# An encoder layer on one core: feed-forward in two phases with its inner activations in DRAM, down projection summed whole in PSUM

## The chip, the cores and the metric

The kernel runs on one core of one Trainium2 chip. The metric is device time in microseconds (us) of one execution. Engines: TensorE (PE, with its weight loads as PEld), VectorE (DVE), ScalarE (ACT), GpSimd (POOL) and SyncE (SP), which issues every DMA of this kernel.

## What is computed

One encoder layer on two inputs with shared weights: a sample of 512 tokens (S) and a prompt of 1,024 tokens (P), width 1,024, all float32.

```
mod = silu(c) @ w_mod + b_mod                       # sh1, sc1, gt1, sh2, sc2, gt2, one vector per input
h = rmsnorm(x, g_norm1) * (1 + sc1) + sh1
q, k, v, xr, gate = split(h @ w_in)                 # 512, 128, 128, 512, 512
attn = banded_attention(q, k, v, sink)              # 8 heads, blocks of 128, window 128
lru = rglru_bidir(xr, ...) * gelu(gate)             # convolution, gates, forward and backward scan
x = x + gt1 * (concat(rmsnorm(attn), rmsnorm(lru)) @ w_out)
h = rmsnorm(x, g_norm2) * (1 + sc2) + sh2
g_, u_ = split(h @ w_ffn_in)                        # 2 x 2816 columns
x = x + gt2 * ((silu(g_) * u_) @ w_ffn_out)
y = rmsnorm(x, g_final)
```

## The kernel before

**Layout and arithmetic.** Activations are held transposed, 128 channels by 512 tokens in a tile; 512 tokens are a chunk, so S has one and P two. To keep float32 accuracy each operand of a large product is split into a high part (float32r) and a low part, `lo = x - hi`, and a product is three matmuls of 128x512: high by high, high by low, low by high (`mm3`). ACT (or DVE, as `Either` picks) makes the high part, DVE the low part. A weight tile is 128x1024 (512 KB): it is loaded into one of 3 stages (`wst`), split into `whi` and `wlo` (10 buffers) and used by 24 matmuls for each chunk. 8 k-blocks of 128 make up the width; the feed-forward has 22 blocks of 128 inner channels (NFF = 22).

**Order of work.** The program is written out at build time. A main generator issues the matmuls of the large products; after each few matmuls `Side.weave` lets other work in: the drains of finished PSUM tiles (`side.soon`, kept in a fast list), one step each of weight load, high and low split (`Weights.pump`), then steps of side generators (norms, modulation chunks `mod_chunk`, attention, `lru`). A step is issued when a cost model (`Plan`) says that its inputs are there at the time that PE has reached, and none while the model has ACT, DVE or POOL far behind PE (`behind`). `Side.finish` issues all that is left of a side generator before the main one goes on; nothing of the main work is issued in that time. Each engine then runs its instructions in that order.

**The stages.** `start` (modulation chunks 0 to 3, S's first norm), `z_main(0)` (h @ w_in of S, 14 weight tiles) beside P's first norm and the modulation chunks 4 to 9, `z_main(1)` (the same for P, both chunks for each weight tile) beside S's recurrence and attention, which are two side generators; after 11 of its tiles both are finished, S's `mixnorm` runs beside two more, then `out_main(0)` (S's product with w_out), the last z tile beside S's `norm2`, and the feed-forward of S. Beside that run P's attention, then P's `lru`, then `mixnorm` of P's first chunk, one after the other in one side generator. They are finished, and `out_main` of P's chunks, `norm2` and the feed-forward of P follow, with the final norm (`final`) at the end of each chunk.

**The feed-forward before** (`ffn`, `ffn_steps`) goes through the inner blocks once. A step "in" makes gate and up of one block (48 matmuls for each chunk), and `gate` and `up` drain them, the product `sg` is split into `ach` and `acl`, in SBUF. After every two blocks a step "out" multiplies them with their two tiles of w_ffn_out, for each of the 8 output blocks m into a fresh PSUM bank, and `drain` adds the part to x, which stays in SBUF:

```
self.dve.scalar_tensor_tensor(out=x, in0=ps, scalar=self.modT[:, seq, 40 + m:41 + m], in1=x,
                              op0=ALU.mult, op1=ALU.add)
```

That is 11 x 8 drains for a chunk. The last step of P's second chunk is done in two halves of 256 tokens, so that the final norm of the first half runs beside the matmuls of the second. PSUM has 8 banks: 4 for the main work (`pm`), 4 for the side work (`ps`).

## Time and profile before

| | |
|---|---|
| median of 3 runs | 1746.13 us (1744.09 to 1746.81) |
| the profiled execution | 1742.62 us, of which the span from first to last instruction is 1740.8 us |
| mean granted clock of TensorE | 0.978 |
| busy share of the span | PE 95%, PEld 76%, DVE 61%, ACT 40%, POOL 5% |
| moved by DMA | 166.84 MB, mean 96 GB/s |

The busy time of PE is that of pipelined matmuls: one of 128x512 takes 0.39 us from start to end, and starts 0.23 us after the one before. How fast PE works is therefore read from how many matmuls a stretch holds, not from its busy share alone. All lines of code carry the number of one helper, so groups are told apart by the names of their tiles: `pm` is a PSUM tile of the main work, `ps` one of the side work.

### The profile page before, as it was taken

The numbers are of one execution on the slowest core, as the hardware profiler recorded it, in microseconds if no ns is written. First come the engines' busy times: TensorE is split into PE (matmuls) and PEld (weight loads), VectorE is DVE, ScalarE is ACT, GpSimd is POOL, SyncE is SP. The second block draws the span as 40 slices with busy tenths as digits, with TensorE's granted clock in tenths as the row PEclk, the third lists the DMA queues.
The fourth block names the chain that finished last, engine by engine and source line by source line (L and its number), as shares of the span: only waits on it lengthen the run. The fifth ranks groups of instructions, "written<-read, shape, count | busy, mean of one in ns | idle before, by whom it ended". The sixth has DMA issues, their size and how long they took to land.

```text
span 1740.8 us, 19699 instructions
## 1 busy us (share of the span) xinstructions
PE 1651.2 (95%) x7428; PEld 1329.8 (76%) x7428; DVE 1058.5 (61%) x1733; ACT 694.9 (40%) x1135; POOL 95.7 (5%) x164
## 2 busy tenths in 40 slices
PE   7979999998999999999929999999999999999996
PEld 2656888786888887777717888888888888888885
DVE  5764876747887878787899754244244244244257
ACT  3343787525665555745735341111111111111114
POOL 0000111001222100000000000000000000000004
PEclk9988999999999999999959999999999999999999
DMA  8766322244222223233315311111111111111102
GB/s 304 266 249 212 109 91 97 86 144 158 96 63 84 73 91 127 85 115 108 104 37 188 118 46 49 49 49 49 49 49 49 49 49 49 49 49 49 49 0 97
DMA packets 70302, 166.84 MB, mean 96 GB/s; under 512 B 7360, under 2 KB 15808, under 8 KB 70208
## 3 DMA queue, kind: packets, MB, share of 16 engines
q1 hardware_dynamic: 70208, 165.59, 28.3%
q8 instruction: 58, 0.95, 0.2%
q14 instruction: 36, 0.29, 0.1%
HBM read 148.26 MB, written 17.30 MB: 95 GB/s over the span
## 4 chain that ended last, share of the span: by engine, by line
PE 82%; DVE 8%; ACT 4%; DMA 4%; issue 1%; SPq 0%; POOL 0%; POOLq 0%; DVEq 0%; ACTq 0%
PE pm L85 74%; PE ps L85 8%; DVE x L85 1%; DMA mst<-w_mod 1%; ACT ga L85 1%; DVE wlo L85 1%; DVE bc L85 1%; DVE lh L85 1%; DMA wst<-w_in 1%; ACT gs L85 1%; ACT gi L85 1%; DVE hl L85 1%; SPq L85 0%; DVE yo L85 0%; ACT whi L85 0%
## 5 line engine op out<-in xcount | busy, mean ns | idle before, releaser
L85 PE MATMUL pm<-hh,whi 128*128 128x512 f32 x1392 | 551.3, 396 | 1.6 <-ACT hh L85 1.3
L85 PE MATMUL pm<-hl,whi 128*128 128x512 f32 x1392 | 545.0, 391 | 3.5 <-DVE hl L85 3.5
L85 PE MATMUL pm<-hh,wlo 128*128 128x512 f32 x1392 | 544.9, 391 | 2.1 <-DVE wlo L85 2.1
L85 PEld LDWEIGHTS pm<-hh,whi 128*128 128x128 f32 x1392 | 263.1, 189 | 61.1 <-issue 5.8
L85 PEld LDWEIGHTS pm<-hh,wlo 128*128 128x128 f32 x1392 | 262.7, 189 | 58.4 <-DVE wlo L85 2.5
L85 PEld LDWEIGHTS pm<-hl,whi 128*128 128x128 f32 x1392 | 263.2, 189 | 56.9 <-DVE hl L85 4.4
L85 ACT ACTIVATE whi<-wst 128x1024 fp32r<-128x1024 f32 x164 | 168.5, 1051 | 294.1 <-issue 181.5
L85 DVE SCALAR_TENSOR_TENSOR x<-pm,modT,x 128x512 f32<-128x512 f32 (+1 forms) x296 | 212.7, 732 | 104.3 <-PE pm L85 103.6
L85 DVE TENSOR_TENSOR wlo<-wst,whi 128x1024 fp32r<-128x1024 f32 x184 | 223.3, 1228 | 9.4 <-ACT whi L85 8.1
L85 DVE TENSOR_TENSOR sg<-sg,pm 128x512 f32<-128x512 f32 x44 | 30.3, 688 | 321.6 <-PE pm L85 321.6
L85 PE MATMUL pm<-ach,whi 128*128 128x512 f32 (+1 forms) x544 | 211.7, 389 | 6.8 <-DVE x L85 4.8
L85 PE MATMUL pm<-acl,whi 128*128 128x512 f32 (+1 forms) x544 | 208.6, 383 | 0.3 <-DVE acl L85 0.3
L85 PE MATMUL pm<-ach,wlo 128*128 128x512 f32 (+1 forms) x544 | 208.5, 383 | 0.0
L85 ACT ACTIVATE ach<-sg 128x512 fp32r<-128x512 f32 x56 | 35.4, 632 | 270.9 <-DVE sg L85 270.9
L85 PEld LDWEIGHTS pm<-ach,whi 128*128 128x128 f32 x544 | 102.2, 188 | 34.8 <-DVE x L85 13.1
L85 PEld LDWEIGHTS pm<-ach,wlo 128*128 128x128 f32 x544 | 102.2, 188 | 20.3
L85 PEld LDWEIGHTS pm<-acl,whi 128*128 128x128 f32 x544 | 102.3, 188 | 19.4 <-DVE acl L85 0.5
L85 ACT ACTIVATE sg<-pm 128x512 f32<-128x512 f32 x66 | 39.4, 598 | 172.6 <-PE pm L85 172.6
L85 PE MATMUL pm<-mxh,whi 128*128 128x512 f32 x192 | 77.4, 403 | 12.0 <-ACT mxh L85 12.0
L85 PE MATMUL pm<-mxl,whi 128*128 128x512 f32 x192 | 77.0, 401 | 7.6 <-DVE mxl L85 7.6
L85 PE MATMUL pm<-mxh,wlo 128*128 128x512 f32 x192 | 76.1, 396 | 0.0
L85 POOL TENSOR_SCALAR sx<-sx,es 128x384 f32<-128x384 f32 (+1 forms) x96 | 60.0, 644 | 243.7 <-DVE es L85 132.0
(150 smaller groups left out, 1707.5 us busy)
## 6 DMA issues: line engine op xcount, KB each, us to landing
wst<-w_f SPq DMA_DIRECT2D x132, 512.0 KB, 3.6
mst<-w_mod SPq DMA_DIRECT2D x96, 256.0 KB, 5.4
wst<-w_in SPq DMA_DIRECT2D x28, 512.0 KB, 4.3
wst<-w_out SPq DMA_DIRECT2D x24, 512.0 KB, 3.7
x<-x_p SPq DMA_DIRECT2D x32, 256.0 KB, 4.7
x<-x_s SPq DMA_DIRECT2D x16, 256.0 KB, 4.5
y_p<-yo SPq DMA_DIRECT2D x16, 256.0 KB, 2.1
zq<-zo SPq DMA_DIRECT2D x12, 256.0 KB, 2.6
```

The source lines that it names most:

```text
L85: r = fn(*args, **kw)
```

## The change

The feed-forward is cut in two phases. `ffn_in` makes gate and up of all 22 blocks and stores the product `sg` in DRAM (256 KB for each block and chunk). The second phase loads it again (`act_reader`, 3 or 4 blocks ahead), splits it, and sums the down projection over all 22 blocks in PSUM, so that each output block is drained once (`down`). For S this is done for 4 output blocks at a time (`ffn_out_half`, 4 main banks): the first half before P's `out_main`, the second half after it, each with half of each tile of w_ffn_out, and each reading the activations again. For P, `ffn_out` does one chunk after the other with all 8 banks, and reads w_ffn_out once for each chunk; in the second chunk the eighth bank is taken two blocks later, and there are no halves of 256 tokens. x after attention goes to DRAM (`R["dram"]`) and comes back at the end of the second phase; `norm2` works in x's own buffers.

Attention and recurrence of P become two side generators that run side by side, from the start of S's feed-forward on, each with its half of `mixnorm` behind it (`mix_att`, `mix_lru`), for both of P's chunks; both are finished after the first half of S's down projection. For S too the two halves of `mixnorm` go behind their generators; they are finished after 12 z tiles of P rather than 11 and 13, and the last two z tiles stand after `out_main(0)`. The modulation chunks 6 to 9 start after 10 z tiles of P rather than at the start, and their loads are issued at most three at a time. The table of the attention bias moves to four heap tiles; the heap has 76 tiles for 73.

`Weights` is rewritten as a list of `Item`s, each a generator that loads a tile, splits it and gives its buffers back by name; `pump` takes one step of each item that is not done. An item for a plain tile does the same three operations as before. `Plan` reckons 300 GB/s for 360 and 0.6 us for 0.5 for each DMA. `ps` issues waiting work while no side bank is free.

```diff
-N_HEAP = 73
+N_HEAP = 76
...
-            cost, lag = n * outs[0].shape[0] * 4 / 360e3, 2.0
+            cost, lag = n * outs[0].shape[0] * 4 / 300e3, 2.0
...
-            self.at["sp"] = max(self.at["sp"], self.done.get(kw["in_"].tensor.name, 0.0)) + 0.5
+            self.at["sp"] = max(self.at["sp"], self.done.get(kw["in_"].tensor.name, 0.0)) + 0.6
...
-        self.table = c.tile([P, 8, 384], BF16, name="table")
...
-        self.sp.dma_start(out=self.table, in_=self.a["table"])
+        self.table = [self.heap.tile([P, 2, 384], BF16, tag="u", name="table") for _ in range(4)]
...
+            if k > 1:
+                yield ws[k - 2],
...
-    def mixnorm(self, c, AO, L, SQ, mix):
+    def mix_half(self, src, acc, g, mix):
...
+        bc = yield from self.rstd(acc, self.ones_h, cut=True)
+        yield from self.par((piece(j, bc) for j in range(4)), W_N)
+    def mix_att(self, c, AO, mix):
         S = [None]
         yield from self.par((self.square_on(t, S) for t in AO[c]), W_SQ)
...
+        yield from self.mix_half(AO[c], S[0], V_GA, mix)
+    def mix_lru(self, c, L, SQ, mix):
+        yield from self.mix_half(L[c], SQ[c], V_GL, mix)
...
+            R["dram"] = [self.dram.tile([P, CH], F32, name=f"xm{seq}_{c}_{i}", tag=f"xm{seq}_{c}_{i}") for i in range(KT)]
...
+        yield x,
+        self.sp.dma_start(out=R["dram"][m], in_=x)
...
-        yield from self.par((self.modulated_on(R["x"][k], bc, self.A2[:, seq], self.modT[:, seq, 24:32], False, R["h"], k)
+        yield from self.par((self.modulated_on(R["x"][k], bc, self.A2[:, seq], self.modT[:, seq, 24:32], True, R["h"], k)
...
-    def ffn(self, seq, Rs, W, native, early=None, late=None, done=None):
...
+        R["x"] = None
...
-            acts[j, c] = yield from self.split_on(s, "ac")
...
-        def drain(ps, x, m, S, last, n):
-            yield ps,
-            self.dve.scalar_tensor_tensor(out=x, in0=ps, scalar=self.modT[:, seq, 40 + m:41 + m], in1=x,
-                                          op0=ALU.mult, op1=ALU.add)
-            self.pm_done()
...
-        def unit_out(js, c):
-            last = js[-1] == NFF - 1
-            n = CH // 2 if last and native and c == len(Rs) - 1 else CH
-            while any((j, c) not in acts for j in js):
...
+        yield s,
+        self.sp.dma_start(out=dst, in_=s)
...
+    def ffn_in(self, Rs, W, native, acts, ahead):
+        for j in range(NFF):
+            if j == NFF - 2:
+                ahead()
+            ds = [{} for _ in Rs]
+            for half in (0, 1):
+                w = W.pop(("f1", j + half * NFF))
+                for c, R in enumerate(Rs):
+                    ps = yield from self.unit(w, R["h"])
+                    self.side.soon(self.up(ps, ds[c], native, acts[c][j]) if half else self.gate(ps, ds[c], native))
+                    yield
+                W.free(*w)
...
+        def fetch(j):
+            t = self.T("ac")
+            self.sp.dma_start(out=t, in_=acts[j])
+            def cut():
+                yield t,
+                got[j] = yield from self.split_on(t, "ac")
+            self.side.soon(cut())
+        for j in range(ahead):
+            fetch(j)
+        def get(j):
+            if j + ahead < len(acts):
+                fetch(j + ahead)
+            while j not in got:
                 self.side.urge(1)
...
+            return got.pop(j)
...
+    def down(self, ps, x, m, gate, S, apart, done):
+        yield ps, x
+        self.dve.scalar_tensor_tensor(out=x, in0=ps, scalar=gate[:, m:m + 1], in1=x, op0=ALU.mult, op1=ALU.add)
+        done()
+        yield x,
+        t = self.T("sqt")
...
+        yield t,
+        if apart or not S:
+            S.append(t)
+        else:
+            self.dve.tensor_tensor(out=S[0], in0=S[0], in1=t, op=ALU.add)
...
+    def ffn_out_half(self, seq, R, W, get, p, S, ahead=None):
...
+        for i in range(NFF // 2):
+            w = W.pop(("f2", p, i))
+            wh, wl = (t.rearrange("p (j m) -> p j m", m=P) for t in w)
+            if i == NFF // 2 - 2:
+                for m in range(4 * p, 4 * p + 4):
+                    x[m] = self.T("x")
+                    self.sp.dma_start(out=x[m], in_=R["dram"][m])
+            for o in range(2):
+                ah, al = get(2 * i + o)
+                first, last = i + o == 0, 2 * i + o == NFF - 1
+                for m in range(4):
+                    if first:
+                        ps[m] = self.pm()
+                    self.mm3(ps[m], wh[:, 4 * o + m, :], wl[:, 4 * o + m, :], ah, al, first, last)
+                    if last:
+                        self.side.soon(self.down(ps[m], x[4 * p + m], 4 * p + m, self.modT[:, seq, 40:48], S, False,
+                                                 self.pm_done))
+                    if m % 2:
+                        yield
+            W.free(*w)
...
+    def ffn_out(self, seq, R, W, get, late, end, ahead, done):
...
+        ps, ws, av = [None] * KT, {}, {}
+        x = R["x"] = [None] * KT
...
+        def share(j, m):
+            if j == 0:
+                ps[m] = self.pm() if m < 4 else self.ps()
+            sl = slice(m * P, (m + 1) * P)
+            self.mm3(ps[m], ws[j][0][:, sl], ws[j][1][:, sl], *av[j], j == 0, j == NFF - 1)
...
+        for j in range(cut):
+            take(j)
...
                 for m in range(KT):
...
+                    x[m] = self.T("x")
+                    self.sp.dma_start(out=x[m], in_=R["dram"][m])
+            for m in range(KT - 1):
+                share(j, m)
+                if m % 2:
                     yield
...
+            if j >= late:
+                share(j - late, KT - 1)
+                drop(j - late)
+            yield
+        S = []
+        for j in range(cut, NFF):
+            take(j)
+        for m in range(KT):
+            for j in range(cut - late if m == KT - 1 else cut, NFF):
+                share(j, m)
+            self.side.soon(self.down(ps[m], x[m], m, gate, S, end, self.pm_done if m < 4 else lambda m=m: self.shut(ps[m])))
+            yield
+        for j in range(cut - late, NFF):
+            drop(j)
+        self.side.urge(len(self.side.fast))
+        done(slice(0, CH), S)
...
-        CUT1, CUT = 11, 13
-        W = Weights(self, wi + wi[:CUT] + wo + wi[CUT:] + ffn_order(1) + wo + wo + ffn_order(2))
+        CUT1, CUT = 10, 12
...
+        def half_order(p):
+            return [(("f2", p, i), two[i, :, :, p * CH:(p + 1) * CH]) for i in range(NFF // 2)]
...
+        f2 = [(("f2", j), a["w_f2"][j]) for j in range(NFF)]
+        W.order = [(key, W.plain(ap)) for key, ap in (
+            wi + wi[:CUT] + wo + wi[CUT:] + f1_order + half_order(0) + wo + wo + half_order(1))]
+        W.order += [(key, W.plain(ap)) for key, ap in f1_order]
+        W.order += [(key, W.plain(ap)) for key, ap in f2 + f2]
...
-        s_mod, s_mod2 = side.add(mods(4, 5)), side.add(mods(6, 7, 8, 9))
+        s_mod = side.add(mods(4, 5))
...
-        s_lru = side.add(self.lru(0, 1, zS, Ls, SQs))
-        s_att = side.add(self.attention(0, 1, zS, AOs))
-        side.gens = [s_lru, s_att] + [e for e in side.gens if e in (s_mod, s_mod2)]
+        s_lru = side.add(chain(self.lru(0, 1, zS, Ls, SQs), self.mix_lru(0, Ls, SQs, mixS)))
+        s_att = side.add(chain(self.attention(0, 1, zS, AOs), self.mix_att(0, AOs, mixS)))
+        side.gens = [s_lru, s_att] + [e for e in side.gens if e is s_mod]
         side.weave(z_main(1, hP, zP, ZO[:CUT1]))
-        side.finish(s_lru, s_att)
-        s_mix = side.add(self.mixnorm(0, AOs, Ls, SQs, mixS))
+        s_mod2 = side.add(mods(6, 7, 8, 9))
...
-        side.finish(s_mix, s_mod)
+        side.finish(s_lru, s_att, s_mod)
         side.weave(out_main(0, 0, mixS, RS))
         mixS.clear()
         side.finish(s_mod2)
...
-        s_mix = side.add(chain(self.attention(1, 2, zP, AOp), self.lru(1, 2, zP, Lp, SQp),
-                               self.mixnorm(0, AOp, Lp, SQp, mixP[0])))
...
-        side.weave(self.ffn(0, [RS], W, False, lambda: side.finish(s_mod3), None, done_s))
-        side.finish(s_mix)
-        RS["h"] = None
-        s_mix = side.add(self.mixnorm(1, AOp, Lp, SQp, mixP[1]))
+        s_lru = side.add(chain(self.lru(1, 2, zP, Lp, SQp), *(self.mix_lru(c, Lp, SQp, mixP[c]) for c in range(2))))
+        s_att = side.add(chain(self.attention(1, 2, zP, AOp), *(self.mix_att(c, AOp, mixP[c]) for c in range(2))))
...
+        side.weave(self.ffn_in([RS], W, False, actS, lambda: reads.append(self.act_reader(actS[0], 4))))
+        RS["h"], RS["x"] = None, [None] * KT
+        side.finish(s_mod3)
+        accS = []
+        side.weave(self.ffn_out_half(0, RS, W, reads.pop(), 0, accS))
+        side.finish(s_lru, s_att)
         side.weave(out_main(1, 0, mixP[0], RP[0]))
-        side.finish(s_mix, *s_fin)
         mixP[0].clear()
         s_norm = side.add(self.norm2(1, RP[0]))
+        reads.append(self.act_reader(actS[0], 4))
         side.weave(out_main(1, 1, mixP[1], RP[1]))
...
         mixP[1].clear()
-        s_norm = side.add(self.norm2(1, RP[1]))
-        side.weave(self.ffn(1, RP, W, True, None, lambda: side.finish(s_norm), done_p))
+        s_norm2 = side.add(self.norm2(1, RP[1]))
+        side.weave(self.ffn_out_half(0, RS, W, reads.pop(), 1, accS))
+        side.urge(len(side.fast))
+        side.add(self.final(0, slice(0, CH), RS, accS, a["y"][0]))
+        side.finish(s_norm, s_norm2)
+        side.weave(self.ffn_in(RP, W, True, actP, read(0)))
+        for c in range(2):
+            RP[c]["h"] = None
+        for c in range(2):
+            side.weave(self.ffn_out(1, RP[c], W, reads.pop(0), 2 * c, c == 1, read(1) if c == 0 else lambda: None, done_p(c)))
```

## Rows read from the trace of the kernel before

**Rows 1.** Page, the 40 slices: tenths busy of PE, granted clock of TensorE.

```profile
PE   7979999998999999999929999999999999999996
...
PEclk9988999999999999999959999999999999999999
```

**Rows 2.** Windows of the core: length, PE, PEld, DVE, ACT, POOL busy, clock, DMA share, GB/s.

```profile
168.00:348.90 180.90, 178.34 (x842) 147.38 (x840) 137.50 (x278) 131.72 (x240) 25.45 (x46) 1.00 0.31 104
...
403.30:413.00 9.70, 5.44 (x16) 4.09 (x17) 9.70 (x16) 6.42 (x10) 0.00 (x0) 0.82 0.79 252
...
435.00:653.00 218.00, 218.00 (x1103) 184.81 (x1102) 175.21 (x408) 129.86 (x276) 39.30 (x69) 1.00 0.25 81
653.00:870.00 217.00, 208.62 (x897) 166.35 (x895) 176.65 (x246) 132.56 (x184) 2.27 (x6) 1.00 0.34 108
870.00:904.40 34.40, 3.24 (x5) 1.36 (x5) 31.83 (x46) 14.43 (x24) 0.00 (x0) 0.54 0.07 23
904.40:957.00 52.60, 49.78 (x201) 39.39 (x201) 48.39 (x65) 23.21 (x34) 3.16 (x2) 0.94 0.50 170
...
1045.00:1690.00 645.00, 645.00 (x2847) 534.10 (x2846) 238.26 (x298) 105.75 (x138) 0.00 (x0) 1.00 0.14 46
...
413.00:904.40 491.40, 449.90 (x2119) 366.35 (x2117) 399.35 (x732) 288.86 (x509) 44.75 (x80) 0.97 0.29 93
```

**Rows 3.** Windows of the PE matmuls into pm alone: length, busy (count), clock, DMA.

```profile
435.00:653.00 218.00, 166.06 (x677) 1.00 0.25 81
653.00:870.00 217.00, 199.20 (x849) 1.00 0.34 108
```

**Rows 4.** Groups of DVE instructions from 413 to 904.4 us: busy us, mean ns, idle before.

```profile
L85 DVE TENSOR_TENSOR wlo<-wst,whi 128x1024 fp32r<-128x1024 f32 x65 | 79.6, 1234 | 0.5 <-ACT whi L85 0.2
L85 DVE SCALAR_TENSOR_TENSOR x<-pm,modT,x 128x512 f32<-128x512 f32 x88 | 64.0, 745 | 1.0 <-PE pm L85 0.8
...
L85 DVE RECIPROCAL bc<-bc 128x128 f32<-128x128 f32 x8 | 6.6, 902 | 0.8 <-ACT bc L85 0.8
...
L85 DVE TENSOR_TENSOR lh<-lh 128x512 f32<-128x512 f32 x8 | 5.3, 680 | 0.0
```

**Rows 5.** Waits of PE in the whole run: us in total, times, longest.

```profile
PE ps L85 <- ACT ssh L85: 18.8, 1, 18.8
PE ps L85 <- ACT mrow L85: 14.0, 3, 7.4
...
PE pm L85 <- DVE hl L85: 3.5, 3, 3.0
```

**Rows 6.** Timeline of ACT: start, length, and in brackets the idle time before.

```profile
87.05 1.06 ACT L85 ACTIVATE whi<-wst 128x1024 fp32r<-128x1024 f32 x1 [6.43 <-DMA wst<-w_in]
...
125.64 1.06 ACT L85 ACTIVATE whi<-wst 128x1024 fp32r<-128x1024 f32 x1 [6.83 <-DMA wst<-w_in]
```

**Rows 7.** Timeline of SP's queue: start, length, what is issued.

```profile
69.62 9.86 SPq L85 DMA_DIRECT2D mst<-w_mod  x13
```

**Rows 8.** Page, DMA issues: count, KB each, median us from issue to landing.

```profile
wst<-w_f SPq DMA_DIRECT2D x132, 512.0 KB, 3.6
mst<-w_mod SPq DMA_DIRECT2D x96, 256.0 KB, 5.4
...
y_p<-yo SPq DMA_DIRECT2D x16, 256.0 KB, 2.1
```

**Rows 9.** Timeline of PE behind the first of the two waits for mrow.

```profile
100.30 0.63 PE L85 MATMUL pm<-hh,wlo 128*128 128x512 f32 x1
...
104.14 0.63 PE L85 MATMUL pm<-hh,wlo 128*128 128x512 f32 x1
```

**Rows 10.** Timeline of PE: the last matmul of the main work.

```profile
1726.64 0.28 PE L85 MATMUL pm<-ach,wlo 128*128 128x256 f32 x1
```

**Rows 11.** Groups of the whole run: fp32 sums over partitions, the same job as at the end.

```profile
L85 PE MATMUL ps<-sqa,ones_d 128*128 128x512 f32 x2 | 1.1, 644 | 0.0
```

More of the change, by code (lines that the diff above doesn't have):

```diff
@@ L32 @@
 S_BC, S_ROW, S_SH, S_END, S_F32, S_X, S_AF, S_W = 7, 1, 22, 5, 24, 2, 4, 20
-N_HEAP = 73
+N_HEAP = 76
 N_WHL = 10
 N_WST = 3
-def ffn_steps(chunks):
-    every = tuple(range(chunks))
-    steps = [("in", (j,), (c,)) for c in every for j in (0, 1)]
-    for j in range(2, NFF - 2):
-        steps.append(("in", (j,), every))
-        if j >= 2 and j % 2 == 0:
-            steps.append(("out", (j - 2, j - 1), every))
-    last = (NFF - 2, NFF - 1)
-    steps.append(("in", last[:1], every))
-    for c in every:
-        steps.append(("in", last[1:], (c,)))
-        if c == 0:
-            steps.append(("out", (NFF - 4, NFF - 3), every))
-        steps.append(("out", last, (c,)))
-    return steps
-def ffn_tiles(step):
-    kind, js, _ = step
-    return [("f1", j + o) for j in js for o in (0, NFF)] if kind == "in" else [("f2", j) for j in js]
 def run(gen):
@@ L381, in ps @@
     def ps(self):
+        while not self.plan.banks:
+            if self.side.fast:
+                self.side.urge(1)
+            else:
+                self.side.step(min(self.side.gens, key=lambda g: self.plan.when(g[1])))
         self.plan.banks.pop(0)
@@ new lines, in norm2, with act_alloc, gate @@
+        R["x"] = None
+    def act_alloc(self, seq, C):
+        return [[self.dram.tile([P, CH], F32, name=f"ac{seq}_{c}_{j}", tag=f"ac{seq}_{c}_{j}") for j in range(NFF)]
+                for c in range(C)]
+    def gate(self, ps, d, native):
+        yield ps,
+        s = d["s"] = self.T("sg")
+        if native:
+            self.act.activation(out=s, in_=ps, func=AF.Silu)
+        else:
+            self.act.activation(out=s, in_=ps, func=AF.Tanh, scale=0.5)
+            yield s,
+            self.dve.scalar_tensor_tensor(out=s, in0=s, scalar=1.0, in1=ps, op0=ALU.add, op1=ALU.mult)
+        self.pm_done()
+        d["gate"] = True
@@ new lines, in up @@
+    def up(self, ps, d, native, dst):
+        yield lambda: "gate" in d,
+        s = d["s"]
+        yield ps, s
+        if native:
+            self.dve.tensor_tensor(out=s, in0=s, in1=ps, op=ALU.mult)
+        else:
+            self.dve.scalar_tensor_tensor(out=s, in0=s, scalar=0.5, in1=ps, op0=ALU.mult, op1=ALU.mult)
+        self.pm_done()
+        yield s,
[12 more added lines that the diff above has]
+                W.free(*w)
@@ L1214, in z_main @@
                     yield
-                W.free()
+                W.free(*w)
         def out_main(seq, c, mix, R):
             for m in range(KT):
-                yield from self.out_unit(seq, c, m, mix, W.pop(("out", m)), R)
-                W.free()
+                w = W.pop(("out", m))
+                yield from self.out_unit(seq, c, m, mix, w, R)
+                W.free(*w)
                 yield
@@ L1276, in program, with done_p, done @@
-        side.weave(self.ffn(0, [RS], W, False, lambda: side.finish(s_mod3), None, done_s))
-        side.finish(s_mix)
-        RS["h"] = None
-        s_mix = side.add(self.mixnorm(1, AOp, Lp, SQp, mixP[1]))
+        s_lru = side.add(chain(self.lru(1, 2, zP, Lp, SQp), *(self.mix_lru(c, Lp, SQp, mixP[c]) for c in range(2))))
+        s_att = side.add(chain(self.attention(1, 2, zP, AOp), *(self.mix_att(c, AOp, mixP[c]) for c in range(2))))
+        def done_p(c):
+            def done(tok, acc):
+                side.add(self.final(c, tok, RP[c], acc, a["y"][1]))
+                side.pace = side.most = 1
+                side.backlog = c == 0
+            return done
```

292 lines of the change are left out of this document (145 added, 147 removed).

## The prediction, made before the changed kernel ran

> **What bounds the kernel now.** I read the 40 slices first, then windows by stage, then what is in them. In the slices PE is busy nine tenths nearly everywhere, with one hole, the 21st slice, at a clock of 5 tenths, and small dents in the first four [rows 1]. P's feed-forward holds 2847 matmuls in 645 us, 0.2266 us each, at full clock with DVE at 238 of 645 us [rows 2]: nothing but matmuls counts there, and this is the price that I use for one of 128x512. The other stage that matters is S's feed-forward with P's attention and recurrence beside it, 413.0 to 904.4 us. Its 1584 matmuls are worth 358.9 us; it takes 491.4, with DVE busy for 399.4 [rows 2]. In its attention stretch PE is full. In its recurrence stretch 897 matmuls, worth 203.3 us, take 217.0, and then PE stands for 34.4 us, with 5 matmuls in it, while DVE is busy for 31.8 of them [rows 2]: the rest of the recurrence and `mixnorm`, which the program finishes before P's `out_main`. The longest single wait of PE, 18.8 us, lies there [rows 5].
>
> At the start PE waits twice for `mrow`, 14.0 us in all but 0.7 [rows 5]. ACT is late there, because at the head of its queue the copy of a weight tile waits 6.4 and 6.8 us for its load [rows 6], and that load stands behind a burst of 13 modulation loads [rows 7]. Behind the first wait matmuls start 0.427 us apart for nine steps (3.84 us between the two rows), about 1.2 GHz, the lower level, rather than 2.4 [rows 9].
>
> **The change, part by part.** PE's main work stays: the same 6,336 matmuls of 512 columns, or their worth. So the time can come only from stretches in which PE waits.
>
> *Drains.* Of S's 88 drains of the down projection 8 stay, 4 of them before P's `out_main`. Each is 0.745 us of DVE, 64.0 us in S's stage [rows 4]. Of P's 176 (and 8 more for the halves) 16 stay; DVE has 407 us free in 645 there [rows 2], so that saves nothing.
>
> *S's stage as changed.* PE: 44 tiles of 24 matmuls and half of the down projection, 1320 x 0.2266 = 299.1. The side work on PE: 449.9 busy less 358.9 for the main work, less 5.3 that the recurrence stretch is busy beyond its count (208.6 less 203.3), so 85.7 [rows 2]; a check, the attention stretch alone has 218.0 - 677 x 0.2266 = 64.6 [rows 2, 3]. With `mixnorm` of P's second chunk (1) PE needs 386 us. DVE: 399.4 as now, less 64.0 of drains, plus 4 drains with their sums, 4 x (0.745 + 0.680) = 5.7, less 11 weight splits that go behind `out_main`, 11 x 1.234 = 13.6, plus `mixnorm` of the second chunk: 8 reciprocals, 6.6, and 21 others at about 0.70, 14.7 [rows 4]. That is 349 us, 90% of PE's 386. The engine that has to be fed is then DVE. Its share is unknown, so I bound it: 80 to 81% in both stretches of this stage now, with the two kinds of side work one after the other (175.2 of 218.0, 176.7 of 217.0); 92% in the 34 us in which PE stood and only side work ran; 76% in S's own stage, where recurrence and attention already run side by side (137.5 of 180.9) [rows 2]. At 90% or more the stage is PE's 386; at 81% it is 431; at 76%, 459. I take 86%, between the first two, since the two sides fill one another's latencies here and the work asked for is larger than in the 76% row: 406. That leaves 20 us of waits for PE.
>
> *The second half of S's down projection* follows P's `out_main`: 264 x 0.2266 = 59.8, and it covers `norm2` of P. DVE has about 62 us to do in it, so I add 4. Together 406 + 59.8 + 4 = 469.8 for 491.4: **-21.6**. P's `out_main` loses its wait for the rest of `mixnorm`: 904.4 to 957.0 holds 201 matmuls, worth 45.5 of its 52.6 us [rows 2]; I take back 6: **-6**.
>
> *Start.* Chunks 6 to 9 (32 loads) leave it, and three loads at most are out at a time, so the burst before the weight loads goes. The two waits are 13.3 us, the slow matmuls behind them 9 x 0.20 = 1.8 and somewhat more each time: up to 18. I take 15: **-15** (bounds 0, if x's loads keep the queue as full, and -18). The chunks' PE work moves and costs the same.
>
> *Where the four chunks go.* They have 2 z tiles and `out_main(0)`, 288 matmuls or 65 us, plus side work. A load lands 5.4 us after issue [rows 8]; 8 loads at three out take some 15, with sums and transposes 20 us for a chunk, 80 for four. The last may not fit, and `norm2` and all behind it wait at `finish(s_mod2)`: **+4** (bounds 0 and +20, one chunk issued with PE standing).
>
> *z tiles.* S's side work has one tile less of P's (10.9 us) before it must be done: +4. The wait before S's feed-forward, 9.7 us with 16 matmuls [rows 2], of which 3.0 is one wait for `hl` [rows 5], is covered by the second tile: -6. **-2** (bounds -6 and +10).
>
> *DRAM.* Stores and loads of the activations and of x, and 22 tiles of w_ffn_out read twice for P. A 512 KB tile lands in 3.6 us and 256 KB of y in 2.1 [rows 8]; in P's second phase 24 matmuls (5.4 us) need one tile and one activation, read 3 blocks (16 us) ahead, with 1.23 + 0.70 us of DVE. PE covers it: **0**. Without that cover the 22 more low halves would cost 22 x 1.234 = 27 us. SP's queue is one for all, so a load that waits for a buffer holds those behind it; the three stages bound that as now.
>
> *Seam of P's two chunks.* All banks are full when the second chunk starts. The last shares of each output block take 6 matmuls (1.36 us), a drain with its sum 1.43 on DVE, so banks come free nearly in step: **+3**. The Trainium skill (Perfetto Trace Analysis, Optimizing Tensor Performance) speaks against the change here: independent groups of matmuls should rotate through the banks, so that the evacuation of one overlaps the next. Held to it, no evacuation would be hidden at the seam; that is a rival below.
>
> *End.* Before, the last main matmul starts at 1726.6 and the span ends 14.2 us later [rows 10]. After, the second chunk's squares are kept apart, so eight fp32 sums of 512 columns run at the end rather than three of 256: two records each, 0.644 us a record with some overlap [rows 11], about 0.9 each, 7 in all. Then root 0.7, four reciprocals 3.6 [rows 4], six products 4.4, store 2.1 [rows 8], 1 for starts: 19: **+5**.
>
> Sum: -21.6 - 6 - 15 + 4 - 2 + 3 + 5 = -32.6, so 1742.6 - 32.6 = 1710.0 for an execution like the profiled one. That one is 3.5 us below the median of the runs; I say 1712.
>
> **Rivals.**
> 1. *All side work fits under PE* (DVE at 90% or more): S's stage 386, 20 less: 1692. For it: 92% has been seen. Against: only with PE standing, and each drain behind a side step holds a bank.
> 2. *DVE stays at 81%*, the share of this stage today: stage 431, 25 more: 1737. `finish(s_lru, s_att)` then leaves a hole like today's.
> 3. *Side by side is no better than in S's own stage*, 76%: 349 / 0.76 = 459, 53 more: 1765, slower. It decides from 443 us on, a DVE share below 79%. For it: it is the only row with both kinds side by side. Against: there PE was busy 178.3 of 180.9 us, so nobody asked DVE for more. More live tiles in the heap, which make a new tile wait for the last reader of an old one, would bring it about.
> 4. *The four chunks are only moved to a worse place*: +16 at `finish(s_mod2)`: 1728.
> 5. *Banks*: no drain hidden at the seam, 8 x 1.43 = 11.4, and a slow clock behind it, 2: 1722. This is what the skill's rule would give; this case's trace has no stage with all banks held.
>
> **How the numbers follow.** The forecast (stage at 396 to 420) gets 0.40, rival 1 0.20, rival 2 0.15, rival 3 0.10, rival 4 0.09, rival 5 0.06. The range leaves out rival 3, what lies beyond the far ends of 1 and 2, and no more: 1684 to 1744. A difference of 0.2%, 3.5 us, is about what a measurement of this kernel can tell from none: faster is below 1742.6. All but rival 3 and the far end of rival 2 are faster: 0.87; same 0.03; slower 0.10.
>
> **What the new profile would show.** Right: the 21st slice's hole is gone or under 20 us; DVE at 84% or more from S's feed-forward to P's `out_main`; no wait for `mrow` over 2 us; P's second phase with 0.2266 us a matmul; at most 4 us without a matmul between P's chunks; 19 us behind the last main matmul. Wrong: a long wait of PE for `mxh` or `ssh` before P's `out_main` (rivals 2, 3), for `mrow` before S's `norm2` (4), for `x` at the seam (5), or gaps in P's second phase that end with a DMA. The sum is most at risk from the 86%: each point of it is 5 us.

## The result and the profile after

The changed kernel takes 1695.18 us (median of 4 runs, 1694.47 to 1695.64), the kernel before 1745.11 us on the same chip (4 runs, 1742.60 to 1746.81): a ratio of 0.9715, 95% interval 0.9698 to 0.9731, 49.9 us. Predicted were 1712 (1684 to 1744). The profiled execution took 1694.91 us with a span of 1693.1; the span is 47.7 us shorter.

The page of the kernel after, shares of the span, then the 40 slices of PE and of the granted clock, as in [rows 1]:

```profile
PE 1639.5 (97%) x7384; PEld 1321.6 (78%) x7384; DVE 954.7 (56%) x1552; ACT 707.9 (42%) x1143; POOL 99.6 (6%) x148
...
PE   7998999999999999997999999999999999999996
...
PEclk9999999999999999998999999999999999999998
```

The hole of the 21st slice is gone, and with it the clock of 5 tenths; what is left of it is the 7 in the 19th slice. Windows of the core after, columns as in [rows 2]: S's feed-forward up to P's `out_main`; the hole at its end; P's `out_main`; second half of S's down projection; P's first phase; P's second phase; the end.

```profile
391.00:801.40 410.40, 391.49 (x1873) 322.02 (x1872) 348.06 (x655) 283.75 (x508) 61.50 (x84) 0.99 0.41 136
788.10:801.40 13.30, 1.33 (x3) 0.79 (x4) 10.85 (x18) 6.16 (x11) 0.00 (x0) 0.67 0.21 77
801.40:891.30 89.90, 89.90 (x388) 74.17 (x387) 63.38 (x81) 37.31 (x51) 0.00 (x0) 0.97 0.56 185
891.30:951.60 60.30, 60.30 (x268) 49.91 (x267) 41.84 (x55) 28.87 (x40) 0.00 (x0) 1.00 0.60 196
951.60:1431.20 479.60, 479.60 (x2116) 396.82 (x2115) 113.43 (x128) 60.55 (x80) 3.44 (x2) 1.00 0.24 79
1431.20:1671.40 240.20, 240.20 (x1059) 198.59 (x1058) 101.21 (x116) 77.65 (x97) 3.42 (x2) 1.00 0.45 152
1671.40:1693.10 21.70, 7.07 (x17) 2.85 (x16) 10.21 (x11) 2.54 (x4) 3.35 (x2) 0.78 0.25 97
```

S's stage holds 348.06 us of DVE in 410.4. From 801.4 to 1671.4 PE is never short of work; P's 2112 matmuls of the first phase take 0.2271 us each, the 1056 of the second 0.2275, side work included. The waits of PE after, columns as in [rows 5]:

```profile
PE ps L61 <- ACT ssh L61: 12.0, 1, 12.0
PE ps L61 <- DMA mst<-w_mod: 8.2, 6, 4.9
PE ps L61 <- ACT mrow L61: 4.4, 4, 2.8
```

The one long wait is for `ssh`. It is the hole; here is its end in the timeline of all engines after (start, length, idle time before in brackets; weight loads left out):

```profile
786.74 2.73 DVE L61 SCALAR_TENSOR_TENSOR ao<-ao,vec,bc 128x512 f32<-128x512 f32 x4
...
794.67 2.49 DVE L61 TENSOR_TENSOR mxl<-ao,mxh 128x512 fp32r<-128x512 f32 x4
795.16 2.17 ACT L61 ACTIVATE sqt<-ao 128x512 f32<-128x512 f32 x4
797.08 2.27 DVE L61 TENSOR_TENSOR sqt<-sqt 128x512 f32<-128x512 f32 x3
799.39 0.63 ACT L61 ACTIVATE ssh<-sqt 128x512 fp32r<-128x512 f32 x1 [2.06 <-DVE sqt L61]
800.05 0.69 DVE L61 TENSOR_TENSOR ssl<-sqt,ssh 128x512 fp32r<-128x512 f32 x1 [0.69 <-ACT ssh L61]
800.07 0.79 PE L61 MATMUL ps<-ssh,ones_h 128*128 128x512 f32 x1 [12.01 <-ACT ssh L61]
800.80 0.79 PE L61 MATMUL ps<-ssl,ones_h 128*128 128x512 f32 x1
801.39 0.63 PE L61 MATMUL pm<-mxh,whi 128*128 128x512 f32 x1
```

The `mxl` at 794.67 are the operands of P's first chunk, which `out_main` needs. What PE waits for at 800.07 is the sum of squares of the second chunk's `ao`, which `out_main` of the first chunk does not need: it stands in PE's order ahead of it, because the two chains that `finish` empties go through `mix_lru` and `mix_att` of both chunks.

**Where the time came from.** S's feed-forward drains its first gate tile at 417.8 us before and at 396.4 after; its 24 matmuls (5.4 us) counted back, the stage starts at 412.4 and 391.0. With that boundary, and P's `out_main` before taken from 904.4 as in the prediction:

| part | before, us | after, us | difference | predicted |
|---|---|---|---|---|
| up to S's feed-forward (start, four chunks, z tiles) | 412.4 | 391.0 | -21.4 | -13 |
| S's feed-forward and the second half of its down projection | 492.0 | 410.4 + 60.3 | -21.3 | -21.6 |
| P's `out_main` | 98.3 | 89.9 | -8.4 | -6 |
| P's feed-forward (DRAM, seam) | 724.2 | 719.8 | -4.4 | +3 |
| behind the last main matmul | 13.9 | 21.7 | +7.8 | +5 |
| sum | | | -47.7 | -32.6 |

### The profile page after: what moved, and what is told of

Its sections match the earlier page's. It is cut to its first block, busy times and chain, and to the rows that moved or that the text cites. A ratio compares the mean times of both kernels' runs of the same rounds, so it can differ in the third digit from the quotient of the medians.

```text
span 1693.1 us, 19983 instructions
## 1 busy us (share of the span) xinstructions
PE 1639.5 (97%) x7384; PEld 1321.6 (78%) x7384; DVE 954.7 (56%) x1552; ACT 707.9 (42%) x1143; POOL 99.6 (6%) x148
## 4 chain that ended last, share of the span: by engine, by line
PE 80%; ACT 5%; DVE 3%; issue 1%; DMA 0%; POOL 0%; DVEq 0%; SPq 0%; ACTq 0%
PE pm L61 66%; PE ps L61 14%; ACT ga L61 1%; ACT gi L61 1%; ACT gs L61 1%; DVE bc L61 0%; ACT L61 0%; DMA mst<-w_mod 0%; DVE xc L61 0%; DVE lh L61 0%; DVE sqt L61 0%; DVE yo L61 0%; ACT whi L61 0%; DVE ao L61 0%; ACT sx L61 0%
## 5 line engine op out<-in xcount | busy, mean ns | idle before, releaser
L61 DVE TENSOR_TENSOR wlo<-wst,whi 128x1024 fp32r<-128x1024 f32 x206 | 252.3, 1226 | 65.6 <-ACT whi L61 61.4
L61 DVE CAST whi<-wst 128x1024 fp32r<-128x1024 f32 x54 | 37.3, 691 | 201.0 <-PE pm L61 194.7
L61 PE MATMUL pm<-ach,whi 128*128 128x512 f32 x352 | 138.3, 393 | 0.2 <-DVE sg L61 0.2
L61 PE MATMUL pm<-ach,wlo 128*128 128x512 f32 x352 | 137.1, 390 | 0.0
L61 PE MATMUL pm<-acl,whi 128*128 128x512 f32 x352 | 137.1, 390 | 0.0
L61 DVE TENSOR_TENSOR acl<-ac,ach 128x512 fp32r<-128x512 f32 x88 | 60.5, 695 | 83.8 <-ACT ach L61 83.6
L61 ACT ACTIVATE ach<-ac 128x512 fp32r<-128x512 f32 x84 | 52.3, 630 | 87.0 <-DMA ac<-ac 86.0
L61 PEld LDWEIGHTS pm<-ach,whi 128*128 128x128 f32 x352 | 66.1, 188 | 14.1 <-DVE sg L61 0.6
L61 PEld LDWEIGHTS pm<-ach,wlo 128*128 128x128 f32 x352 | 66.1, 188 | 13.9
L61 PEld LDWEIGHTS pm<-acl,whi 128*128 128x128 f32 x352 | 66.1, 188 | 13.3 <-issue 0.2
```

The lines of the kernel that those rows point to most:

```text
L61: r = fn(*args, **kw)
```

## The experiments

Medians are of four runs each. The kernel before ran beside each group and came out between 1742.4 and 1745.1, so the kernels are compared by what each gains on the one beside it; the kernel after gains 49.9 us. "Leftover" is the time between the last matmul of the down projection's first half (in kernels built on the one before, the whole of S's feed-forward) and the first of P's `out_main`, in which PE has only side work left; it is read from the end and the start of these matmuls. The windows below have rounded edges and can hold a little more.

| kernel | median, us | ratio to before, 95% | gain, us | leftover, us |
|---|---|---|---|---|
| after | 1695.18 | 0.9698 to 0.9731 | 49.9 | 13.3 |
| e1_seq | 1751.67 | 1.0030 to 1.0060 | -8.1 | 80.4 |
| e2_mods_early | 1713.13 | 0.9811 to 0.9840 | 30.5 | 17.7 |
| e3_dve_extra | 1715.86 | 0.9829 to 0.9858 | 27.8 | 35.3 |
| e4_tail | 1693.97 | 0.9701 to 0.9733 | 49.6 | 13.3 |
| e5_before_mods_late | 1733.85 | 0.9931 to 0.9964 | 10.1 | 32.2 |
| e6_plan_old | 1707.80 | 0.9777 to 0.9806 | 36.2 | 12.0 |
| e7_mix_split | 1680.62 | 0.9623 to 0.9651 | 63.4 | 0 |
| e9_both | 1676.51 | 0.9598 to 0.9626 | 67.5 | 0 |
| e10_before_side | 1734.66 | 0.9931 to 0.9961 | 10.4 | 11.5 |
| e11_drains | 1729.57 | 0.9902 to 0.9931 | 15.5 | 52.6 |
| e12_cut9 | 1680.31 | 0.9608 to 0.9643 | 64.8 | 0 |
| e13_four_out | 1686.99 | 0.9669 to 0.9701 | 55.4 | 0 |

### S's stage: the order of the side work

**e1_seq**: the kernel after with one chain in place of two.

```
-        s_lru = side.add(chain(self.lru(1, 2, zP, Lp, SQp), *(self.mix_lru(c, ...) for c in range(2))))
-        s_att = side.add(chain(self.attention(1, 2, zP, AOp), *(self.mix_att(c, ...) for c in range(2))))
+        s_lru = s_att = side.add(chain(self.attention(1, 2, zP, AOp), self.lru(1, 2, zP, Lp, SQp),
+                                       *(self.mix_lru(c, ...) for c in range(2)), *(self.mix_att(c, ...) for c in range(2))))
```

> Edit: in the changed kernel P's attention, recurrence and mixnorm are one side generator again, one after the other; all else stays. Theory A (DVE has to be kept fed, and the two sides fill one another's latencies): DVE's share of S's feed-forward stage falls from 84.8% to about 81%, the share of the kernel before, so its 348 us take 430 rather than 410, and the hole before P's out_main grows from 12 to 30 us or more: 1715 us, between 1708 and 1725. Rival B (the drains that went are the whole gain of that stage, the order of the side work is indifferent): within 4 us of the changed kernel's 1695.

It lost all of the gain and 8.1 us more, 58 us against the kernel after, far beyond both theories. Windows of e1_seq: the stage, then its leftover.

```profile
391.00:857.60 466.60, 394.52 (x1873) 323.57 (x1872) 346.26 (x652) 283.29 (x505) 47.64 (x80) 0.92 0.36 119
777.00:857.60 80.60, 12.87 (x26) 5.87 (x26) 52.85 (x74) 45.19 (x69) 0.00 (x0) 0.53 0.06 21
```

DVE's work is that of the kernel after (346 us for 348), its share falls from 85 to 74%. All of the loss stands behind the last main matmul at 777: the rest of the recurrence up to 817, some 40 us, then the four normalizations one after the other, whose sums follow each other by 10 to 15 us, another 40 us. PE waits 57.5 us in four waits for `ssh`. The experiment sets recurrence and normalizations of both chunks in one row at once, so it does not tell what each change of the order costs by itself.

**e10_before_side**: the kernel before with `lru` and `attention` side by side, and `mixnorm` of the first chunk when both are done (W_B 2 for 3).

```
-        s_mix = side.add(chain(self.attention(1, 2, zP, AOp), self.lru(1, 2, zP, Lp, SQp), self.mixnorm(0, ...)))
+        side.add(chain(self.lru(1, 2, zP, Lp, SQp), mark()))
+        side.add(chain(self.attention(1, 2, zP, AOp), mark()))
+        s_mix = side.add(after_both())        # mixnorm(0, ...) once both marks are set
```

> The kernel before, with the side work of S's feed-forward reordered alone: P's recurrence and attention side by side instead of one after the other, mixnorm of the first chunk when both are done; at most two instead of three of the recurrence's inner groups at a time (W_B 2 for 3), since the activations still lie on chip and leave less room. Drains, weights and the start as before. Theory A (the order of the side work is the gain in this stage, whatever DVE carries): DVE's 399 us at the 85% that the stage of the kernel after reached, 471 us for 495.6, so about 20 to 25 us below the kernel before, 1718 to 1724. Theory B (side by side needs the drains and the activations out of the way, the first for DVE, the second for room): within 6 us of the kernel before, or slower.

Between the two: 10.4 us. Windows of e10_before_side, stage and leftover:

```profile
411.00:897.40 486.40, 456.86 (x2132) 371.76 (x2132) 403.13 (x735) 293.89 (x517) 56.52 (x84) 0.98 0.31 98
885.00:897.40 12.40, 0.90 (x5) 0.40 (x4) 11.23 (x18) 3.31 (x7) 0.00 (x0) 0.64 0.27 94
```

The leftover falls from 32.2 us, the hole of [rows 2] by this measure, to 11.5 (the window opens 0.9 us before the last main matmul ends): the order, with the smaller W_B, fills most of it. But with 403 us of DVE the work ahead of it takes 474 us, and the stage starts some 9 us later than before (first gate drain at 426.6 us for 417.8). That may be the smaller W_B in S's own recurrence; it was not tried by itself.

**e11_drains**: the kernel after, but S's down projection is drained into `x` after each pair of blocks.

```
             av = [get(2 * i), get(2 * i + 1)]
             for m in range(4):
                 ps = self.pm()
                 for o in range(2):
                     self.mm3(ps, wh[:, 4 * o + m, :], wl[:, 4 * o + m, :], *av[o], o == 0, o == 1)
                 self.side.soon(drain(ps, 4 * p + m))       # the last block pair: self.down(...)
```

> The kernel after, but S's down projection is drained from PSUM into x after each pair of blocks, as before: 40 more drains of about 0.745 us, 30 us of DVE, in the first half ahead of P's out_main and as many in the second half behind it. All else as after. Theory A (DVE's work ahead of out_main decides the stage, as 30 us of other DVE work there cost 20.7): the hole of 13.3 us grows to 30 or more and the time to 1712 to 1722. Theory B (what counts is the order of the side work, and drains find room between it): within 5 us of the kernel after.

Theory A, and dearer than it said: 34 us. Windows of e11_drains, stage and leftover:

```profile
391.70:837.10 445.40, 403.39 (x1874) 327.03 (x1873) 369.98 (x687) 290.17 (x516) 52.69 (x84) 0.96 0.38 125
784.50:837.10 52.60, 25.85 (x107) 17.64 (x105) 37.85 (x95) 29.54 (x68) 8.21 (x16) 0.73 0.09 30
```

DVE has 22 us more ahead of `out_main`, the leftover grows by 39, and 107 matmuls of side work now stand in it that the kernel after had done beside the down projection. The edit also holds four tiles of x from the start of each half; what that costs by itself was not tried.

**e3_dve_extra**: the kernel after with two more additions on DVE for each of S's 22 gate tiles, whose result nothing reads (30.4 us).

```
         self.pm_done()
+        if not native:
+            for _ in range(2):
+                yield s,
+                self.dve.tensor_tensor(out=self.T("dd"), in0=s, in1=s, op=ALU.add)
```

> Edit: in S's first phase DVE adds each block's product to itself twice into a tile that nobody reads, 44 more adds of 128x512, 30 us of DVE at 0.69 us each, nothing else; the output stays the reference's. Theory A (DVE is what S's feed-forward stage waits for): the stage grows by what DVE needs at its share of 85%, 25 to 36 us: 1720 to 1731. Rival B (PE's own 386 us and the latencies of the side chains set the stage, DVE's 15% of idle time takes the adds): 1695 to 1703.

Between the two and near A, which said 25 to 36 us: 22 us. The first phase, in which the additions run, ends no later (707.0 us, after 710.3); what they push back comes out in the leftover. Window of e3_dve_extra, the leftover:

```profile
787.60:822.90 35.30, 13.75 (x39) 7.37 (x38) 24.52 (x51) 17.54 (x34) 4.15 (x8) 0.60 0.09 30
```

**e7_mix_split**: the kernel after, the second chunk's normalization issued beside the first `out_main`.

```
-        s_lru = side.add(chain(self.lru(1, 2, zP, Lp, SQp), *(self.mix_lru(c, Lp, SQp, mixP[c]) for c in range(2))))
+        s_lru = side.add(chain(self.lru(1, 2, zP, Lp, SQp), self.mix_lru(0, Lp, SQp, mixP[0])))
...
+        s_mix = [side.add(self.mix_lru(1, Lp, SQp, mixP[1])), side.add(self.mix_att(1, AOp, mixP[1]))]
         side.weave(out_main(1, 0, mixP[0], RP[0]))
+        side.finish(*s_mix)
```

> The kernel after, but the normalization of P's second chunk (mix_lru and mix_att of c = 1) is no longer in the chains that must be done before P's first out_main; it is issued beside that out_main and finished behind it. Theory A (the 13.3 us hole before out_main is the second chunk's normalization standing in PE's order ahead of out_main, whose own operands are ready earlier): hole 4 to 7 us, time 6 to 9 us below the kernel after, 1686 to 1689. Theory B (the hole is the last of the attention and recurrence themselves, or the normalization only moves behind out_main and opens a hole there): within 3 us of the kernel after.

Theory A's place, and more than its size: 13.5 us, the whole hole. Windows of e7_mix_split, S's stage and P's `out_main`:

```profile
391.70:788.30 396.60, 389.73 (x1871) 321.56 (x1870) 331.09 (x630) 277.14 (x497) 60.10 (x84) 1.00 0.42 138
788.30:877.00 88.70, 88.70 (x392) 73.37 (x391) 77.25 (x106) 42.96 (x63) 0.00 (x0) 1.00 0.58 199
```

17 us of DVE move behind the stage, where `out_main` covers them. The expectation left 4 to 7 us for the first chunk's own end; with less queued in the chains that is done inside the down projection too. The stage is now PE's alone.

### The start: the chunks and the planner

**e5_before_mods_late**: the kernel before with the late, paced chunks alone.

```
+            if k > 1:
+                yield ws[k - 2],
...
-        s_mod, s_mod2 = side.add(mods(4, 5)), side.add(mods(6, 7, 8, 9))
+        s_mod = side.add(mods(4, 5))
...
+        s_mod2 = side.add(mods(6, 7, 8, 9))
         side.weave(z_main(1, hP, zP, ZO[CUT1:CUT]))
```

> The kernel before, with one part of the change alone: the modulation chunks 6 to 9 are issued before the last z tiles instead of at the start, and each chunk's loads go out at most three at a time; all else as before. Theory A (the late and paced chunks alone are the gain at the start, as the prediction's term has it): the two waits for mrow, 13.3 us, go, and the time is 13 to 18 us below the kernel before, about 1728. Theory B (the gain at the start needs what else changed there, one z tile of P fewer before S's side work must be done, the new planner constants, the weights' new loader): less than 6 us below the kernel before.

Between the theories, 10.1 us: one of the two waits for `mrow` is gone, the other is 4.6 us long.

**e6_plan_old**: the kernel after with the planner's two constants for a DMA put back.

```
-            cost, lag = n * outs[0].shape[0] * 4 / 300e3, 2.0
+            cost, lag = n * outs[0].shape[0] * 4 / 360e3, 2.0
...
-            self.at["sp"] = max(...) + 0.6
+            self.at["sp"] = max(...) + 0.5
```

> The kernel after, with the planner's two constants for a DMA put back (360e3 for 300e3, 0.5 for 0.6). Theory A (the constants decide nothing): within 3 us of the kernel after, 1692 to 1698, with no wait for mrow over 3 us. Theory B (the constants keep the weight loads ahead of the modulation loads, so the waits for mrow come back with the old ones): mrow waits of 8 us or more and a time of 1703 or more.

Theory B: 13.7 us, with 10.1 us of waits for `mrow`. These two numbers only decide where the program's writer puts an instruction.

**e2_mods_early**: the kernel after with chunks 6 to 9 issued at the start, unpaced, as before.

```
-        s_mod = side.add(mods(4, 5))
+        s_mod, s_mod2 = side.add(mods(4, 5)), side.add(mods(6, 7, 8, 9))
...
-        s_mod2 = side.add(mods(6, 7, 8, 9))
```

(and without the two lines that pace the loads)

> Edit: the modulation chunks 6 to 9 go back to the start of the program, beside S's z tiles, with their eight loads issued in a burst as before; all else stays. Theory A (the burst ahead of the weight loads makes ACT late at the start): the two waits for mrow come back, 13 us with 4 us of matmuls at the low clock, while the 6 us that PE stands for the last chunk behind out_main go: 1695 + 12 = 1707, between 1702 and 1717. Rival B (the start gains from the planner's dearer DMA or from the rewritten weight loads): within 4 us of 1695, no wait for mrow over 3 us.

The time is A's, 19.4 us, the mechanism isn't. SP's queue in e2_mods_early shows the burst again, at the place of that of [rows 7] (the row there holds the 13 loads in its window; the burst of the kernel before has 16 too, from 67.81, in 11.67 us):

```profile
68.89 11.61 SPq L61 DMA_DIRECT2D mst<-w_mod  x16
```

ACT is late as before: its copy of the weight tile waits 6.02 us for the load (6.43 in [rows 6]), and `mrow` is copied at 94.07, 1.2 us earlier than before (95.24). The timeline of ACT in e2_mods_early:

```profile
88.08 1.06 ACT L61 ACTIVATE whi<-wst 128x1024 fp32r<-128x1024 f32 x1 [6.02 <-DMA wst<-w_in]
...
94.07 1.07 ACT L61 ACTIVATE mrow<-ps 128x512 f32<-128x512 f32 x2
```

But PE, at the place of the first of the two waits, does not wait, since it still has z tiles to do until then. The timeline of PE in e2_mods_early:

```profile
96.19 1.84 PE L61 MATMUL ps<-sel,mrow 128*128 128x2 f32 x16
```

In the kernel before the same 16 matmuls start at 95.87 behind a wait of 7.36 us and take 3.57. All waits for `mrow` are 3.1 us here. With a burst and the old constants PE waits 13.3 us at these two places, nearly all of the 14.0 of [rows 5]; with paced loads and the old constants 5.0 (e5) and 4.7 (e6); with the new constants 0 with the burst (e2) and 0.3 with paced loads (after). The timeline of PE in e6_plan_old at the first place, and in the kernel after:

```profile
106.90 1.87 PE L61 MATMUL ps<-sel,mrow 128*128 128x2 f32 x8 [4.27 <-ACT mrow L61]
```

```profile
106.81 0.95 PE L61 MATMUL ps<-sel,mrow 128*128 128x2 f32 x8
```

The second such step stands at 132.33 in e6 and at 167.17 in the kernel after. What e2 costs instead are the chunks' own matmuls, which stand earlier in PE's order (the z tiles ahead of S's `out_main` end at 326.3 us for 311.1), and then a wait of 7.1 for `mxh`: S's feed-forward starts 11.9 us later. Another 4.4 us stand in the leftover; the last 3 were not traced. First gate drains of S's feed-forward: before 417.8, e5 409.2, e2 408.3, e6 406.5, after 396.4.

### The end, and what is left at the start

**e4_tail**: in P's second chunk the squares are summed on DVE, as in the first, and one fp32 sum stands at the end (the argument `c == 1` becomes `False`).

> Edit: in P's second chunk the eight squares are added up on DVE as in the first chunk, so that one fp32 sum over partitions runs at the end rather than eight. Theory A (the eight sums, 7.0 us behind the last main matmul, lie on the path that ends last): 5 to 6 us less, one sum of 0.9 us and one add of 0.7 stay: 1690, between 1688.5 and 1691.5. Rival B (the adds make DVE late for the last drains, which need 0.75 us of every 1.36, and the end moves as much): 1694 to 1696.

B: no difference that can be measured. PE waits 3.83 us for the last DVE sum, in place of the seven sums that it no longer makes. The timeline of PE in e4_tail:

```profile
1674.85 2.07 PE L61 MATMUL ps<-sqt,ones_d 128*128 128x512 f32 x2 [3.83 <-DVE sqt L61]
```

**e9_both**: e7, and only the last two of eight squares kept apart.

```
-        if apart or not S:
+        if not S or apart and m > 5:
             S.append(t)
```

> The edit of e7 and a shorter end: in P's second chunk only the last two output blocks keep their squares apart, the first six are summed on DVE, so that three fp32 sums instead of eight stand at the end. Theory A (both gains are real and lie in different places): 3 to 4 us below e7, about 1683. Theory B (as where all squares were summed on DVE, the sum's latency eats what the shorter row of sums gives): within 2 us of e7.

A: 4.1 us below e7, and 67.5 below before: 18 us better than the kernel after. The timeline of PE in e9_both, with three sums of two matmuls:

```profile
1655.53 1.02 PE L61 MATMUL ps<-sqt,ones_d 128*128 128x512 f32 x2
1656.75 1.98 PE L61 MATMUL ps<-sqt,ones_d 128*128 128x512 f32 x4 [0.20 <-ACT sqt L61]
```

The first sum lies before the last square is there; a wait of 0.2 us is all that is left.

**e12_cut9** and **e13_four_out** go after the 6.5 us between S's `out_main` and the next z tile, in which PE does the last chunk. The one issues the chunks a z tile earlier (`CUT1, CUT = 9, 12`), the other lets four loads out at a time (`if k > 2: yield ws[k - 3],`), both on e9.

> The kernel of e9, with the modulation chunks 6 to 9 issued behind P's 9th z tile instead of its 10th (CUT1 9 for 10). Theory A (the 6.2 us between S's out_main and the next z tile, where PE waits for the last chunk's loads, go, since the chunks have one z tile, 10.9 us, more): 3 to 6 us below e9, about 1671 to 1673. Theory B (the loads wait on SP's queue behind other work and the chunks end as late, or they delay S's side work as the early chunks did): within 2 us of e9, or slower.

> The kernel of e9, with up to four instead of three modulation loads of a chunk out at a time. Theory A (the chunks 6 to 9 are paced by their loads, three at a time, and PE's 6.2 us between S's out_main and the next z tile are the last of these): the 6.2 us go or shrink to under 2, and the time is 4 to 6 us below e9, 1671 to 1673. Theory B (SP's queue and the heap are the limit, or four loads at once push the weight loads back at the start): within 2 us of e9, or slower.

B both times: e12 gains nothing (2.7 us slower than e9, with intervals that overlap and four runs over 6.7 us), e13 is 12.1 us slower. The stretch is gone in both, but its work stands elsewhere. The timeline of PE in the kernel after shows why there was little to gain:

```profile
361.73 1.91 PE L61 MATMUL ps<-mst,caw 128*32 128x512 f32 x12
364.99 1.71 PE L61 MATMUL ps<-mst,caw 128*32 128x512 f32 x4 [1.34 <-DMA mst<-w_mod]
367.39 1.05 PE L61 MATMUL ps<-sel,mrow 128*128 128x2 f32 x8 [0.69 <-ACT mrow L61]
```

4.7 of the 6.5 us are matmuls of the chunk, which must be done somewhere. In e13_four_out 9.4 us of waits for `mrow` and one of 4.2 for `mx` come back; why four loads bring them is not settled.

## Why the prediction was right, and where not

**The sum.** The sign and the main term held and the time lies in the range; it came 15.1 us below the sum of 1710.0 in an execution of the same kind. Of these 8.4 come from the start, 7.4 from P's feed-forward and 2.4 from `out_main`; the end took 2.8 back.

**S's stage** was priced at 469.8 us and took 470.7. Its parts are nearly as worked out: DVE 348 us (349), stage 410.4 (406), second half 60.3 (63.8), share 85% (86%). As a mechanism the share is weaker than as a number, and that the stage came out so close is partly luck. Where the two kinds of side work run side by side the share is 83 to 86% in four kernels whose DVE work differs by up to 55 us (after, e3, e11, e10), so 86%, taken from between 80 and 92, was close. But a share in the eighties does not by itself mean that PE waits: in e7 DVE is busy for 331 of 396.6 us, 83%, and there is no hole. Where its 20 us of waits would lie, the sum did not say. Beside the main work PE goes on with few gaps, busy for 390 of 397 us in the kernel after and for 378 of 393 in e11, and nearly all of the loss stands in one piece behind it, as a chain that nothing covers: 13.3 us after, 35.3, 52.6 and 80.4 in e3, e11 and e1. More work for DVE makes that piece longer (e3, e11), and so does another order with the same work (e1). Rival 1, all of it under PE, needed one edit more (e7): 396.6 us, of which PE is busy 389.7, with its own need worked out at 386.

**Rival 3, slower**, was said to decide below a share of 79%. e1 is that case: 74%, and 8.1 us slower than before. What would bring it about was looked for in the heap; it came from the order instead. For rival 2, one kind after the other, I took 81% and 431 us from the kernel before; e1 took 466.6, since in that row the normalization of one chunk only stood ahead of `out_main`.

**Neither half of the change carries the gain.** Without the order (e1, where the normalization of the second chunk stands in the row too) the whole sum in PSUM loses 8 us against before, with the gain of the start counted in; without the whole sum for S (e11) 15.5 of the 49.9 us stay, less than the start alone gave.

**The start** is the step that was mis-sized, -21.4 for -13, and its reason was half right. The chunks moved and paced are worth 8.6 us at S's first gate drain (e5); the planner's constants, which I left out of the account, 10.1 (e6 against after). The remaining 2.7 of the 21.4 us were not parted further. The burst was there in both kernels, with the wait and without it (e2): where the step stands in PE's order decides whether a late load is seen. Of the smaller terms, the chunks' new place cost some 2 us (6.5 between S's `out_main` and the next z tile, 4.7 of them matmuls of the chunk) rather than 4, and rival 4's 16 did not come; the 4 us for one z tile fewer did not come either, since S's `out_main` starts 0.6 us behind the z tile ahead of it (311.7 for 311.1).

**P's feed-forward** has no gap at the seam, where I put 3 us. The window of the kernel after around it:

```profile
1545.00:1557.00 12.00, 12.00 (x53) 9.61 (x52) 9.99 (x15) 6.67 (x10) 0.00 (x0) 1.00 0.13 50
```

All eight banks are held for some 120 us by one chunk, but its eight groups end one after the other, so the drain of a block, 0.75 us, runs beside the last shares of the blocks behind it, 1.36 us each in other banks. The Trainium skill (Perfetto Trace Analysis, Optimizing Tensor Performance) asks that independent groups of matmuls rotate through the banks, so that the evacuation of one overlaps the matmuls of the next. The trace agrees with that; it was wrong to read it as speaking against the change. Rival 5 cost nothing. DRAM cost nothing either: 231 MB moved for 167, and no wait of PE in P's second phase. The other 4.4 us of the stage were in no term. They lie in the last step of the kernel before, with its halves of 256 tokens: its stretch from 1690.0 to 1726.9 us holds 92 matmuls of 512 columns and 102 of 256, worth 32.4 us at 0.2266 and half of it, and takes 36.9.

**The end** was predicted at 19 us and took 21.7. The timeline of the kernel after:

```profile
1671.44 7.03 PE L61 MATMUL ps<-sqt,ones_d 128*128 128x512 f32 x16
...
1678.57 0.69 ACT L61 ACTIVATE bc<-ps,eps 128x512 f32<-128x512 f32 x1 [5.51 <-PE ps L61]
...
1679.28 3.39 DVE L61 RECIPROCAL bc<-bc 128x128 f32<-128x128 f32 x4 [6.89 <-ACT bc L61]
1682.71 6.07 DVE L61 SCALAR_TENSOR_TENSOR yo<-x,vec,bc 128x512 f32<-128x512 f32 x6
1682.89 3.35 POOL L61 TENSOR_TENSOR yo<-x,bc 128x512 f32<-128x512 f32 x2 [107.30 <-issue]
```

The sums (7), the root (0.7) and the reciprocals (3.4 for 3.6) are near their prices. The products are not: 6.07 for 4.4 us; and from the last product to the end it takes 4.3 us, where store and starts were put at 3.1.

**Signs.** The hole under 20 us, DVE at 84% or more and the seam came as said. So did one sign of being wrong: PE waits 12.0 us for `ssh` before P's `out_main`, which was to mean rival 2 or 3. With a hole of 13.3 us it meant neither; the two lists overlap there. One wait for `mrow` of 2.8 us is left where none over 2 was to be; it belongs to chunks 10 and 11, inside S's feed-forward.

## What to carry to other kernels

Where side work must be done before the main work can go on, ask of each instruction in the emptied queue whether the next main step needs it: 17 us of DVE's work for the second chunk stood in such a queue and cost 13.3, which one edit gave back. A share of an engine's time forecasts such a stage only within one order of the work; look at the piece that is left when the cover ends, and price it as a chain. Pace and place of loads are set by the model that writes the order, so a change of its constants is a change to be priced like any other.

## What was unexpected of the hardware

Two of the six products that DVE makes at the end took 1.75 and 1.74 us, the other four 0.74 to 0.75. The two are those that started while POOL was at one of its own two products (1.69 and 1.70 us), and each ended some 0.5 us after that one did: at 1685.12 for 1684.58, and at 1686.79 for 1686.24. The same is seen at S's end, 1.78 and 1.77 for 0.74. In the kernel before, with products of 256 columns, three of the four in each half started beside POOL's and took 0.94 to 0.95 us, the fourth 0.49. The Trainium skill (GPSIMD Engine Reference, 1. Specifications) says that POOL's access to SBUF is shared with VectorE, and that DVE instructions with two inputs in SBUF contend with it; these products read `x` and `bc` from there, and the durations agree with that rule. No run here takes POOL's products away, so the cause is not shown.
